# Moving weight splits, weight loads and the last norm of a hybrid decoder layer on one Trainium2 core

## The chip, the cores and the metric

The kernel runs on one core of one Trainium2 chip. TensorE (PE) does the matmuls; VectorE (DVE), ScalarE (ACT) and GpSimd (POOL) do elementwise work, each in the order of its own queue; SyncE (SP) issues most DMA transfers, also in queue order, so that whatever stands behind a waiting instruction waits too. The metric is the device time of one execution in microseconds (us). The kernel before took 1433.9 us, the median of 3 runs from 1433.82 to 1433.96.

## The reference

One decoder layer in float32, sequence S = 1024, width D = 1024, feed-forward width 2816, one batch. Cut to its frame (the details of the attention branches are left out):

```python
n1 = rms_norm(h, g_mix[i])
proj = n1 @ w_in[i]
...
mixed = jnp.concatenate([rms_norm(y_conv, g_gn_conv[i]), rms_norm(y_attn, g_gn_attn[i])], axis=-1)
h = h + mixed @ w_out[i]
u = causal_dwconv(rms_norm(h, g_ffn[i]) @ w_up[i], w_ffn_conv[i])
u_gate, u_val = jnp.split(u, 2, axis=-1)
h = h + (jax.nn.silu(u_gate) * u_val) @ w_down[i]
ple_gate = jax.nn.sigmoid(rms_norm(h, g_ple[i]) @ w_ple_gate[i])
h = h + ple_gate * (p[i] @ w_ple_proj[i])
return rms_norm(h, g_final)
```

`rms_norm` divides by the root of the mean square of a row and multiplies by a gain.

## The kernel before

Activations lie with the features on the partitions: eight tiles `hx0` to `hx7` of 128 features by 1024 tokens hold the residual stream, and a stage works on halves of 512 tokens. Every float32 product is made of three matmuls (`mm3`, lines 180 to 182): a high part times a high part and two mixed terms. Each weight and each moving operand is therefore *split* before use: ACT copies the high part (line 101) and DVE subtracts it from the original to get the low part (line 104). A split has two halves on two engines, and the second needs the first.

Weights come through a plan. `fetch` issues a load into a raw tile (line 147; line 142 for the weights `pt` of the last gate), `send` splits it, and `weights(key)` runs `send` a few keys ahead of use. The tiles come from pools with a fixed number of buffers per tag: `opool` has the tags `or` (raw) and `ot` (4 buffers, also used for temporaries), the feed-forward pool has `fp` pages, the general pool `pg` pages. A tile waits until the readers of the buffer's last holder are done. The program is written in the order of the calls, but a scheduler places each instruction on its engine's queue; `behind(a, b)` adds an edge, without a semaphore, that keeps a after b in that order.

The stages that matter, in order of time:

1. *Output product* (`oc` to 552 us, `oa` to 614 us). `conv_out` multiplies the convolution group by `out00` to `out07` (PE tile `oc`). `out_half(1)` and `out_half(0)` multiply the normalised attention group `yan` by `out10` to `out17` (PE tile `oa`, eight tiles for each half of the tokens, 12 matmuls each), DVE adds the result to `hx` (line 966), ACT and DVE take sums of squares (`facc`), and SP writes the half tile to DRAM (`hd`, line 968). `hold_out` splits `out1x` into one page `out1x_p` that holds both parts. Ahead of the loop stand loads and splits of the layer's embedding operands: `pT` (`ptr`, `pth`, `ptl`) and `w_pp` (`ppr`, `pph`, `ppl`). `norm0` is the group norm for the second half of the tokens; after its rsqrt (ACT `an0rr`, behind an ACT_TABLE_LOAD) come the four `yan0x` splits.
2. *Embedding* (614 to 638 us). `embed()` multiplies `pT` by `w_pp` in eight steps of 12 matmuls and parks the result in DRAM. After six steps the sum of the feed-forward norm (`fn0s`) goes to PE; its reciprocal and transpose on DVE give `fn0rb`.
3. *Feed-forward up* (636 to 1082 us). The products go by Strassen-like combinations: seven moving operands `m1` to `m7` (splits of sums and differences of the four normed quarters `x11`, `x12`, `x21`, `x22`) and, for each of the 22 column pairs j, seven weight combinations made by `up_weights(j)`: `ug` (products 1 and 2), `ut` (5 and 6), `us` (3 and 7), `uv` (4), with sums on DVE (lines 984 to 987). PE accumulates in `ua`, `ub`, `uc`, `ud`; `up(j)` convolves, applies SiLU and writes `ad`.
4. *Feed-forward down* (1062 to 1324 us, beginning between the last up products): PE tile `d`, weights `down0j` and `down1j`, 512 KB each, activations `a` read back from `ad`. The raw tiles of `pt` have buffers of the tags `or` and `ot`, which the up stage uses until its end.
5. *Gates* (1325 to 1417 us). Column gates `g` with weights `pg`, then for the last 256 tokens the gate `gl` by token with weights `pt`. The final norm of tokens 0 to 767 (`on`, generator `final`) is a sum, a rsqrt (ACT square root and DVE reciprocal unless its name is in `NEWTON`, where DVE does twelve small instructions), a transpose to `onrb`, and eight multiplications of `h` (line 1236) that each release an output DMA on POOL's queue (line 1237). The tokens 768 to 1023 (`hT6`, `hT7`) are finished by `gated` and `norm` (lines 1302 to 1327).

## Time and profile before

| | before |
|---|---|
| median of 3 runs | 1433.9 us |
| profiled execution, its own time | 1434.68 us |
| span of that execution | 1432.9 us |
| PE busy | 1379.8 us, 96% of the span |
| DVE, ACT, POOL busy | 927.4, 629.6, 130.5 us |
| mean granted TensorE clock | 0.985 of 2.4 GHz |

"Busy" counts executing instructions. A row of the trace gives start, duration, engine, line, operation, output<-input and shape; in square brackets stands the idle time of the engine just before it and what ended it. PEclk is the share of full speed that TensorE was granted. A share near 100% says which engine to look at, not where time can be had: that is read from the places where that engine stands still, and from what ends each wait.

### The profile page before, as it was taken

How to read it: one execution, taken by the hardware profiler on the slowest of the kernel's cores; microseconds unless marked ns; L12 is line 12 of the kernel's file. 1: busy time of each engine (PE TensorE's matmuls, PEld its weight loads, DVE VectorE, ACT ScalarE, POOL GpSimd, SP SyncE). 2: the span in 40 equal slices, each digit the busy share in tenths (PEclk: the TensorE clock that was granted, in tenths of full speed). 3: DMA queues.
4: the chain of work that ended last, by engine and by line, in shares of the span. 5: the costliest groups of instructions: out<-in, count | busy, mean ns of one | idle time of the engine just before them, and what ended most of it. 6: DMA issues, size and time to landing. Idle time of an engine off the chain costs nothing.

```text
span 1432.9 us, 17553 instructions
## 1 busy us (share of the span) xinstructions
PE 1379.8 (96%) x6527; PEld 1086.8 (76%) x6527; DVE 927.4 (65%) x1655; ACT 629.6 (44%) x1032; POOL 130.5 (9%) x147
## 2 busy tenths in 40 slices
...
GB/s 266 112 183 119 90 59 30 30 89 30 12 34 79 26 81 155 81 184 37 87 82 88 75 88 89 59 88 74 89 221 247 134 143 108 200 109 81 118 98 174
DMA packets 68773, 148.64 MB, mean 104 GB/s; under 512 B 6608, under 2 KB 28112, under 8 KB 68688
## 3 DMA queue, kind: packets, MB, share of 16 engines
...
q0 software_dynamic: 640, 3.15, 0.6%
...
## 4 chain that ended last, share of the span: by engine, by line
PE 87%; DVE 5%; DMA 3%; SPq 2%; ACT 1%; issue 1%; POOL 0%; DVEq 0%; POOLq 0%; ACTq 0%
PE d L180 6%; PE d L181 6%; PE d L182 6%; PE ua L182 4%; PE ua L181 4%; PE ua L180 4%; PE uc L182 3%; PE uc L181 3%; PE uc L180 3%; PE sy L755 2%; PE wy L755 2%; PE g L180 2%; PE g L182 2%; PE g L181 2%; PE ud L180 1%; PE ud L182 1%
## 5 line engine op out<-in xcount | busy, mean ns | idle before, releaser
L180 PE MATMUL d<-a,down_h 128*128 128x512 f32 x352 | 139.8, 398 | 4.4 <-ACT down_h L101 4.4
L181 PE MATMUL d<-a,down_h 128*128 128x512 f32 x352 | 139.5, 396 | 0.0
L182 PE MATMUL d<-a,down_l 128*128 128x512 f32 x352 | 136.5, 394 | 0.0
L104 DVE TENSOR_TENSOR down_l<-down_r,down_h 128x1024 fp32r<-128x1024 f32 x44 | 53.9, 1224 | 111.5 <-ACT down_h L101 68.0
L101 ACT ACTIVATE down_h<-down_r 128x1024 fp32r<-128x1024 f32 x44 | 46.7, 1061 | 137.1 <-DMA down_r<-in_w_down_dram 120.9
L1237 POOL DMA_DIRECT2D out_dram<-h x8 | 4.5, 564 | 865.0 <-DVE h L1236 864.8
L180 PEld LDWEIGHTS d<-a,down_h 128*128 128x128 f32 x352 | 66.7, 190 | 21.1 <-ACT down_h L101 5.2
L181 PEld LDWEIGHTS d<-a,down_h 128*128 128x128 f32 x352 | 66.7, 189 | 15.5
L182 PEld LDWEIGHTS d<-a,down_l 128*128 128x128 f32 x352 | 66.1, 188 | 15.7
L1143 ACT ACTIVATE uc<-xg,vec 128x1024 f32<-128x1024 f32 x22 | 25.3, 1151 | 107.1 <-DVE xg L1136 107.1
L1136 DVE TENSOR_TENSOR xg<-uc,e 128x512 f32<-128x512 f32 x22 | 15.2, 691 | 73.9 <-PE uc L182 73.7
L101 ACT ACTIVATE in_h<-in_r 128x1024 fp32r<-128x1024 f32 (+1 forms) x20 | 20.7, 1037 | 95.0 <-PE cx L181 30.1
L707 ACT ACTIVATE ps<-ps,stat 128x512 f32<-128x512 f32 (+7 forms) x64 | 49.1, 770 | 13.4 <-DVE stat L718 13.1
L104 DVE TENSOR_TENSOR in_l<-in_r,in_h 128x1024 fp32r<-128x1024 f32 (+2 forms) x22 | 25.0, 1140 | 28.8 <-ACT in_h L101 28.7
L180 PE MATMUL g<-gh,pg_h 128*128 128x512 f32 (+1 forms) x128 | 43.5, 340 | 0.0
L182 PE MATMUL g<-gh,pg_l 128*128 128x512 f32 (+1 forms) x128 | 43.2, 337 | 0.0
L181 PE MATMUL g<-gl,pg_h 128*128 128x512 f32 (+1 forms) x128 | 43.1, 337 | 0.0
L104 DVE TENSOR_TENSOR a<-a 128x512 fp32r<-128x512 f32 x44 | 28.8, 687 | 20.2 <-ACT a L101 20.0
L626 ACT ACTIVATE pw<-pw,stat 128x640 f32<-128x640 f32 (+3 forms) x56 | 38.2, 685 | 5.5 <-DVE stat L680 3.3
L101 ACT ACTIVATE uth<-ut 128x1024 fp32r<-128x1024 f32 x22 | 23.4, 1063 | 37.2 <-DVE ut L985 37.2
L180 PE MATMUL oa<-yan,out_p 128*128 128x512 f32 x64 | 28.0, 438 | 11.4 <-ACT out_p L101 6.3
L566 PE MATMUL s<-ks,qa 128*128 128x512 f32 (+3 forms) x96 | 36.5, 387 | 0.2 <-DVE stat L718 0.2
...
## 6 DMA issues: line engine op xcount, KB each, us to landing
down_r<-in_w_down_dram SPq DMA_DIRECT2D x44, 512.0 KB, 4.4
uvr<-in_w_up_dram SPq DMA_DIRECT2D x22, 512.0 KB, 3.6
ugr<-in_w_up_dram SPq DMA_DIRECT2D x22, 512.0 KB, 4.5
ad<-uc SPq DMA_DIRECT2D x22, 512.0 KB, 2.8
...
in_r<-in_w_in_dram SPq DMA_DIRECT2D x18, 512.0 KB, 7.1
qa<-qd SPq DMA_DIRECT2D x8, 512.0 KB, 4.8
...
```

What stands on the lines that cost most here:

```text
L101: nc.scalar.activation(hi, x, AF.Copy)
L104: (nc.gpsimd if (lo_eng or lo_of[0]) == "pool" else nc.vector).tensor_sub(lo, x, f32(hi))
L180: first = nc.tensor.matmul(ps, wh, mh, start=start, stop=False, **more)
L181: nc.tensor.matmul(ps, wh, ml, start=False, stop=False, **more)
L182: return first, nc.tensor.matmul(ps, wl, mh, start=False, stop=stop, **more)
L566: nc.tensor.matmul(ps[:, c0:c0 + n], b.qa[:, h, :], k, start=True, stop=False)
L626: nc.scalar.activation(w[:, :b.nw * P], w[:, :b.nw * P], AF.Exp, bias=b.M_W[:, h:h + 1], scale=-1.0, accum_out=b.D_W[:, h:h + 1])
L707: nc.scalar.activation(w[:, :nk], w[:, :nk], AF.Exp, bias=b.M_S[:, h:h + 1], scale=-1.0, accum_out=b.D_S[:, h:h + 1])
L755: m = nc.tensor.matmul(py[64 * g:64 * g + 64, :], vals(n, g), pts[g], start=n == 0, stop=n == nblk - 1)
L1136: nc.vector.tensor_add(xg[:, hi], c, e2)
L1143: nc.scalar.activation(u, xe[:, 0:S], AF.Copy, scale=col(tap))
L1237: nc.gpsimd.dma_start(out[k], o)
```

## The change

Line numbers in the rows are those of the program they belong to; lines of the changed kernel stand 0 to 19 higher.

1. `hold_out`: `out10` and `out11` go to four `ot` tiles (`out10_h`, `out10_l`, ...) in place of pages; `out12` to `out14` (before: `out10` to `out13`) use the feed-forward pool, the rest general pages.
2. The loads and splits of `pT` and `w_pp` are issued after two steps of `out_half(1)`, `norm0`'s first step and two more steps, where before they stood ahead of all of them.
3. `fetch` puts each `pt` load behind the last load issued for another weight (`sent_load`).
4. `up_weights` becomes a generator: first the loads and the split of `ug`, then the sums and the other splits. For pair 1 the second step is issued after all moving operands; for all other pairs both follow one another as before. The moving operands come in the order 6, 5, 7, 4, 3 (before 7, 6, 5, 4, 3) and differ in which temporaries they use.
5. `fn0s` is issued after four steps of `embed()` instead of six.
6. `final`: `on` joins `NEWTON`; the first step is issued behind the last column gate, the second (with its matmul behind the latest `gl` matmul) after the third `pt0` weight, the rest after the loop.

```diff
@@ -111,9 +111,13 @@
     def hold_out(key, raw):
 
         c = int(key[4:])
-        t = wpage([P, 2, 512], f"{key}_p", F32R) if c < 4 else page([P, 2, 512], f"{key}_p", F32R)
-        split(raw, t[:, 0], t[:, 1])
-        parts_of[key] = (t[:, 0], t[:, 1])
+        if c < 2:
+            parts = [opool[0].tile([P, 512], F32R, tag="ot", name=f"{key}_{u}", bufs=4) for u in "hl"]
+        else:
+            t = wpage([P, 2, 512], f"{key}_p", F32R) if c < 5 else page([P, 2, 512], f"{key}_p", F32R)
+            parts = [t[:, 0], t[:, 1]]
+        split(raw, *parts)
+        parts_of[key] = parts
 
     def split_gain(x, g, hi, lo):
         nc.scalar.activation(hi, x, AF.Copy, scale=g)
@@ -124,6 +128,7 @@
     order, src_of, raw_of, parts_of, got, sent = [], {}, {}, {}, [0], [0]
     hold = {"out00", "out10", "down00"}
     with_raw = {}
+    sent_load = [None]
 
     def plan(key, src, n):
         order.append(key)
@@ -139,12 +144,12 @@
             elif key.startswith("pt"):
                 raw = [opool[0].tile([P, 512], F32, tag=t, name=f"{key}_r{u}", bufs=b) for u, (t, b) in enumerate((("or", 2), ("ot", 4)))]
                 for u in range(2):
-                    load(raw[u], src[:, hs(u)])
+                    behind(load(raw[u], src[:, hs(u)]), sent_load[0])
                 raw_of[key] = raw
                 continue
             else:
                 raw = rawpage([P, n], f"{key}_r")
-            load(raw, src)
+            sent_load[0] = load(raw, src)
             raw_of[key] = raw
 
     def send(upto):
@@ -979,14 +984,16 @@
         load(v, w_up[2 * j + 1])
         load(g, w_up[2 * j])
         one, two = hs(0), hs(1)
+        gh_, gl_ = (wpage([P, S], f"ug{q}{j}", F32R) for q in "hl")
+        split(g, gh_, gl_)
+        ups[j] = {1: (gh_[:, one], gl_[:, one]), 2: (gh_[:, two], gl_[:, two])}
+        yield
         t = page([P, S], f"ut{j}")
         a7, a3 = (opool[0].tile([P, 512], F32, tag="or", name=f"u{q}s{j}", bufs=2) for q in "73")
         nc.vector.tensor_add(t[:, two], v[:, one], v[:, two])
         nc.vector.tensor_add(t[:, one], g[:, one], t[:, two])
         nc.vector.tensor_add(a7, g[:, one], v[:, one])
         nc.vector.tensor_add(a3, g[:, two], t[:, one])
-        gh_, gl_ = (wpage([P, S], f"ug{q}{j}", F32R) for q in "hl")
-        split(g, gh_, gl_)
         th_, tl_ = (wpage([P, S], f"ut{q}{j}", F32R) for q in "hl")
         split(t, th_, tl_)
         sh_, sl_ = (wpage([P, S], f"us{q}{j}", F32R) for q in "hl")
@@ -994,9 +1001,9 @@
         vp = wpage([P, S], f"uv{j}", F32R)
         split(v[:, two], vp[:, one], vp[:, two])
         split(a3, sh_[:, two], sl_[:, two])
-        ups[j] = {1: (gh_[:, one], gl_[:, one]), 2: (gh_[:, two], gl_[:, two]), 6: (th_[:, one], tl_[:, one]),
-                  5: (th_[:, two], tl_[:, two]), 7: (sh_[:, one], sl_[:, one]), 4: (vp[:, one], vp[:, two]),
-                  3: (sh_[:, two], sl_[:, two])}
+        ups[j].update({6: (th_[:, one], tl_[:, one]), 5: (th_[:, two], tl_[:, two]), 7: (sh_[:, one], sl_[:, one]),
+                       4: (vp[:, one], vp[:, two]), 3: (sh_[:, two], sl_[:, two])})
+        yield
 
     mov = {n: [None] * 4 for n in range(1, 8)}
 
@@ -1009,6 +1016,13 @@
         x = h[k][:, hs(hf)]
         nc.vector.scalar_tensor_tensor(x, x, col(V_FFN + k), rb, op0=ALU.mult, op1=ALU.mult)
         return x
+
+    half1, half0 = out_half(1), out_half(0)
+    next(half1)
+    next(half1)
+    next(norm0)
+    next(half1)
+    next(half1)
 
 
     pparts, wppt, wpp = [], [], []
@@ -1027,10 +1041,6 @@
         for c in range(4):
             wpp.append([[t[:, (2 * c + k) * P:(2 * c + k + 1) * P] for k in range(2)] for t in wppt[q]])
 
-    half1, half0 = out_half(1), out_half(0)
-    next(half1)
-    next(half1)
-    next(norm0)
     for _ in half1:
         pass
     res1 = []
@@ -1040,7 +1050,8 @@
         next(half0)
     next(norm1)
     x12, x22 = ([normed(k + 4 * q, 1, res1[0]) for k in range(4)] for q in range(2))
-    up_weights(0)
+    for _ in up_weights(0):
+        pass
     for _ in half0:
         pass
 
@@ -1073,7 +1084,7 @@
 
     mark = []
     steps = embed()
-    for _ in range(6):
+    for _ in range(4):
         next(steps)
     rb = rstd_rows([fsum[0]], D, "fn0", sums=lambda m: (behind(m, last[0]), mark.append(m)))
     for _ in steps:
@@ -1084,25 +1095,25 @@
     x21 = [normed(k + 4, 0, rb) for k in range(4)]
     for k in range(4):
         moving(2, k, x21[k])
-    up_weights(1)
-    for k in range(4):
-        t = temp(f"t7{k}")
-        nc.vector.tensor_sub(t, x22[k], x12[k])
-        moving(7, k, t)
-    x6 = []
+    second = up_weights(1)
+    next(second)
     for k in range(4):
         nc.vector.tensor_sub(x11[k], x11[k], x12[k])
-        t = x12[k]
+        t = temp(f"t6{k}")
         nc.vector.scalar_tensor_tensor(t, x11[k], -1.0, x22[k], op0=ALU.mult, op1=ALU.subtract)
         moving(6, k, t)
-        x6.append(t)
+        nc.vector.tensor_add(x21[k], x21[k], t)
     for k in range(4):
         moving(5, k, x11[k])
     for k in range(4):
-        nc.vector.tensor_add(x21[k], x21[k], x6[k])
+        nc.vector.tensor_sub(x12[k], x22[k], x12[k])
+        moving(7, k, x12[k])
+    for k in range(4):
         moving(4, k, x21[k])
     for k in range(4):
         moving(3, k, x22[k])
+    for _ in second:
+        pass
 
     def product(ps, j, n, start=True):
 
@@ -1158,7 +1169,8 @@
             next(run[j])
         next(run[j])
         if j + 2 < NF:
-            up_weights(j + 2)
+            for _ in up_weights(j + 2):
+                pass
         if j == NF - 2:
             hold.clear()
             send(order.index("down01") + 1)
@@ -1230,7 +1242,7 @@
     def final(acc):
 
         res = []
-        yield from rstd_steps(res, [acc], D, "on")
+        yield from rstd_steps(res, [acc], D, "on", sums=lambda m: behind(m, last[0]))
         for k in range(KC):
             o = h[k][:, 0:LAST]
             nc.vector.scalar_tensor_tensor(o, o, col(V_FIN + k), res[0], op0=ALU.mult, op1=ALU.mult)
@@ -1278,6 +1290,7 @@
                     nc.tensor.transpose(ps[:, k * P:(k + 1) * P], h[4 * q + k][:, toks[i]], ident)
                 nc.scalar.activation(hT[i][:, hs(q)], ps, AF.Copy)
     done = final(acc)
+    next(done)
 
 
     gfin = page([P, D], "gfin")
@@ -1294,7 +1307,7 @@
         for k in ks:
             o = (k % 2) * 512 + c0 % 512
             wh, wl = (t[0][:, o:o + n] for t in wgt[c0 // 512, k // 2])
-            mm3(ps, gh[k][:, toks[i]], gl[k][:, toks[i]], wh, wl, k == 0, k == KC - 1)
+            last[0] = mm3(ps, gh[k][:, toks[i]], gl[k][:, toks[i]], wh, wl, k == 0, k == KC - 1)[1]
 
     def gated(i, c0, n, pg, last):
         cs = slice(c0, c0 + n)
@@ -1332,6 +1345,8 @@
         wgt[0, kk] = weights(f"pt0{kk}", width=KC * P)
         for i in late:
             token_product(pgs[i], i, 0, 512, (2 * kk, 2 * kk + 1))
+        if kk == 2:
+            next(done)
     for kk in range(4):
         wgt[1, kk] = weights(f"pt1{kk}", width=KC * P)
     for i in late:
@@ -1340,19 +1355,17 @@
         for c0, n in pieces[i, 1]:
             pg = bank(f"gl{i}{c0}")[:, 0:n]
             token_product(pg, i, c0, n, range(KC))
-            if done:
-                for _ in done:
-                    pass
-                done = None
             used[i] = gated(i, c0, n, pg, (i, c0, n) == (late[-1], *pieces[i, 1][-1]))
             if i != late[-1]:
                 norm(i, used[i])
+    for _ in done:
+        pass
     norm(late[-1], used[late[-1]])
 
 
 LAST = 768
 GAP = (1, 4, 5)
-NEWTON = ("cn", "an1", "o6")
+NEWTON = ("cn", "an1", "on", "o6")
 OUT2 = (P, (S - LAST) // P, D)
 NPB, NPAGE, NWR, NWT, NFP, NPW, NHALF, AHEAD = 4, 29, 2, 8, 18, 13, 8, 3
```

How the queues move, from the order in which each program issues its instructions. First ACT at the start of the output product by `out10` to `out17`; `pth`, `pph` are high parts of `pT` and `w_pp`, `ugh0` the high part of the first up weight, `facc1` and `f11sq` squares, `an0rr` the rsqrt of `norm0`. Before:

```order
L101 ACTIVATE pth0_5077<-ptr0_5075 128x1024
L101 ACTIVATE pth1_5083<-ptr1_5081 128x1024
L101 ACTIVATE pph0_5089<-ppr0_5087 128x1024
L101 ACTIVATE pph1_5095<-ppr1_5093 128x1024
L101 ACTIVATE out10_p_5106<-out10_r_5100 128x512
L101 ACTIVATE out11_p_5109<-out11_r_5102 128x512
L101 ACTIVATE out12_p_5112<-out12_r_5104 128x512
L101 ACTIVATE out13_p_5133<-out13_r_5131 128x512
L210 ACTIVATE facc1_5099<-hx0_4116 128x512
L101 ACTIVATE ugh0_5388<-ugr0_5378 128x1024
L222 ACT_TABLE_LOAD
L222 ACTIVATE an0rr_5156<-an0s_5154,eps_83 128x16
```

The changed kernel, same engine and place:

```order
L101 ACTIVATE out10_h_5082<-out10_r_5076 128x512
L218 ACTIVATE ya01sq_5018<-ya1_2052 128x512
L218 ACTIVATE ya02sq_5021<-ya2_2053 128x512
L218 ACTIVATE ya03sq_5024<-ya3_2054 128x512
L101 ACTIVATE out11_h_5086<-out11_r_5078 128x512
L215 ACTIVATE facc1_5075<-hx0_4116 128x512
L101 ACTIVATE out12_p_5090<-out12_r_5080 128x512
L101 ACTIVATE out13_p_5111<-out13_r_5109 128x512
L227 ACT_TABLE_LOAD
L227 ACTIVATE an0rr_5134<-an0s_5132,eps_83 128x16
L218 ACTIVATE f11sq_5128<-hx1_4380 128x512
L101 ACTIVATE out14_p_5157<-out14_r_5155 128x512
```

The splits of `pT`, `w_pp` and `ugh0` have left the space ahead of `out14_p`; the split of `out14` has moved ahead of the `yan0x` splits.

Then DVE while the up stage starts; `m7x` is a low part of moving operand 7, `t7x` its difference, `ut1`, `u3s1`, `utl1`, `usl1` belong to the weights of pair 1. Before:

```order
L985 TENSOR_TENSOR ut1_5742<-ugr1_5739,ut1_5742 128x512
L1090 TENSOR_TENSOR t72_5776<-hx6_4970,hx2_4512 128x512
L1090 TENSOR_TENSOR t73_5781<-hx7_5031,hx3_4724 128x512
L1096 SCALAR_TENSOR_TENSOR hx0_4116<-hx0_4116,hx4_4812 128x512
L1096 SCALAR_TENSOR_TENSOR hx1_4380<-hx1_4380,hx5_4897 128x512
L104 TENSOR_TENSOR m70_5768<-t70_5766,m70_5768 128x512
L987 TENSOR_TENSOR u3s1_5744<-ugr1_5739,ut1_5742 128x512
L104 TENSOR_TENSOR m71_5773<-t71_5771,m71_5773 128x512
L1096 SCALAR_TENSOR_TENSOR hx2_4512<-hx2_4512,hx6_4970 128x512
L104 TENSOR_TENSOR utl1_5754<-ut1_5742,uth1_5753 128x1024
L1096 SCALAR_TENSOR_TENSOR hx3_4724<-hx3_4724,hx7_5031 128x512
L104 TENSOR_TENSOR m72_5778<-t72_5776,m72_5778 128x512
```

The changed kernel, where the first instruction for `ut1` stands:

```order
L104 TENSOR_TENSOR m30_5816<-hx4_4812,m30_5816 128x512
L104 TENSOR_TENSOR m31_5819<-hx5_4897,m31_5819 128x512
L104 TENSOR_TENSOR m32_5822<-hx6_4970,m32_5822 128x512
L104 TENSOR_TENSOR m33_5825<-hx7_5031,m33_5825 128x512
L993 TENSOR_TENSOR ut1_5828<-uvr1_5740 128x512
L994 TENSOR_TENSOR ut1_5828<-ugr1_5741,ut1_5828 128x512
L996 TENSOR_TENSOR u3s1_5830<-ugr1_5741,ut1_5828 128x512
L104 TENSOR_TENSOR utl1_5836<-ut1_5828,uth1_5835 128x1024
L104 TENSOR_TENSOR usl1_5840<-u7s1_5829,ush1_5839 128x512
```

The instructions for `ut1`, `u3s1`, `utl1` stood between those for the moving operands and now stand behind the last one, `m33`.

Last SP where the down stage starts; `a0xx` are activations read back, `ad<-uc120` writes those of pair 20, `downxx_r` are down weights. Before:

```order
L1173 DMA a018_9472<-ad_5072 128x512
L1149 DMA ad_5072<-uc119_8659 128x1024
L1173 DMA a019_9508<-ad_5072 128x512
L142 DMA pt00_r1_10923<-in_w_pt_dram 128x512
L142 DMA pt01_r1_11013<-in_w_pt_dram 128x512
L142 DMA pt02_r1_11090<-in_w_pt_dram 128x512
L142 DMA pt03_r1_11211<-in_w_pt_dram 128x512
L147 DMA down02_r_8924<-in_w_down_dram 128x1024
L1149 DMA ad_5072<-uc120_8784 128x1024
L147 DMA down03_r_8958<-in_w_down_dram 128x1024
L1173 DMA a020_9544<-ad_5072 128x512
```

The changed kernel:

```order
L1185 DMA a018_9474<-ad_5072 128x512
L1185 DMA a019_9510<-ad_5072 128x512
L1160 DMA ad_5072<-uc120_8786 128x1024
L152 DMA down02_r_8926<-in_w_down_dram 128x1024
L1185 DMA a020_9546<-ad_5072 128x512
```

The four `pt` loads have gone from here (they now stand behind the last column-gate weight `pg7_r`), and `down02_r` has moved from ahead of the write of pair 20 to behind it.

## Rows read from the trace of the kernel before

**Rows 1.** The page of the profile: busy time, share and instructions of each engine, and the chain of work that ended last, by engine.

```profile
PE 1379.8 (96%) x6527; PEld 1086.8 (76%) x6527; DVE 927.4 (65%) x1655; ACT 629.6 (44%) x1032; POOL 130.5 (9%) x147
PE 87%; DVE 5%; DMA 3%; SPq 2%; ACT 1%; issue 1%; POOL 0%; DVEq 0%; POOLq 0%; ACTq 0%
```

**Rows 2.** Waits of PE over the whole span, grouped: matmul tile and line, what ended the wait, then us in total, times, longest.

```profile
PE oa L180 <- ACT out_p L101: 6.3, 1, 6.3
PE oa L180 <- DVE hx L966: 5.0, 1, 5.0
PE d L180 <- ACT down_h L101: 4.4, 1, 4.4
PE uc L180 <- ACT m L101: 1.5, 1, 1.5
PE ud L180 <- ACT m L101: 1.1, 1, 1.1
```

**Rows 3.** Stretches of the span: its bounds and length, then busy us (and instructions) of PE, PEld, DVE, ACT, POOL, then PEclk, DMA share and GB/s.

```profile
558.00:563.20 5.20, 4.58 (x11) 3.63 (x12) 2.52 (x5) 1.72 (x4) 0.00 (x0) 0.50 0.35 104
577.40:580.00 2.60, 2.38 (x5) 1.13 (x5) 2.60 (x6) 1.56 (x4) 0.00 (x0) 0.50 0.26 101
580.00:600.00 20.00, 20.00 (x79) 16.06 (x80) 12.36 (x19) 4.95 (x8) 0.00 (x0) 0.90 0.29 105
650.00:655.00 5.00, 2.35 (x6) 1.26 (x6) 5.00 (x12) 3.43 (x7) 0.00 (x0) 0.71 0.52 186
655.00:680.00 25.00, 25.00 (x102) 20.12 (x101) 20.92 (x33) 10.12 (x16) 0.00 (x0) 0.92 0.02 4
1090.00:1095.00 5.00, 5.00 (x18) 3.95 (x18) 3.36 (x4) 2.26 (x3) 0.00 (x0) 0.76 0.81 273
1395.00:1418.00 23.00, 21.86 (x119) 18.62 (x118) 18.37 (x29) 14.10 (x25) 0.83 (x2) 1.00 0.30 107
1418.00:1433.00 15.00, 0.00 (x0) 0.00 (x0) 9.95 (x30) 3.13 (x7) 3.68 (x7) 0.57 0.74 280
```

**Rows 4.** Timeline of ACT in the output product: start, us, instruction, idle before it and what ended that.

```profile
552.86 1.06 ACT L101 ACTIVATE pth<-ptr 128x1024 fp32r<-128x1024 f32 x1 [4.60 <-DMA ptr<-in_pT_dram]
...
555.81 2.23 ACT L101 ACTIVATE pph<-ppr 128x1024 fp32r<-128x1024 f32 x2 [0.20 <-DMA ppr<-in_w_pp_dram]
557.95 1.13 ACT L101 ACTIVATE out_p<-out_r 128x512 fp32r<-128x512 f32 x2
...
568.49 1.06 ACT L101 ACTIVATE ugh<-ugr 128x1024 fp32r<-128x1024 f32 x1 [1.86 <-DMA ugr<-in_w_up_dram]
...
576.79 0.61 ACT L101 ACTIVATE out_p<-out_r 128x512 fp32r<-128x512 f32 x1
```

**Rows 5.** Timeline of DVE in the same place.

```profile
553.94 2.93 DVE L104 TENSOR_TENSOR ptl<-ptr,pth 128x1024 fp32r<-128x1024 f32 x2 [0.80 <-ACT pth L101]
556.90 2.40 DVE L104 TENSOR_TENSOR ppl<-ppr,pph 128x1024 fp32r<-128x1024 f32 x2
```

**Rows 6.** Timeline of PE: the last two matmuls before the wait that begins at 552.28 us.

```profile
551.65 0.39 PE L181 MATMUL oc<-ycl,out_h 128*128 128x512 f32 x1
551.89 0.39 PE L182 MATMUL oc<-ych,out_l 128*128 128x512 f32 x1
```

**Rows 7.** Timeline of DVE from the feed-forward norm to the up stage.

```profile
622.35 0.69 DVE L246 TENSOR_REDUCE fn0red<-fn0tr 128x16 f32<-128x512 f32 x1
...
627.92 0.25 DVE L223 RECIPROCAL fn0rr<-fn0rr 128x16 f32<-128x16 f32 x1 [4.88 <-ACT fn0rr L222]
...
634.26 3.09 DVE L104 TENSOR_TENSOR m<-hx,m 128x512 fp32r<-128x512 f32 x5
...
648.72 1.22 DVE L104 TENSOR_TENSOR utl<-ut,uth 128x1024 fp32r<-128x1024 f32 x1
```

**Rows 8.** Timeline of PE: the first matmul with weights `ut` of pair 0, behind the first four product tiles.

```profile
648.73 0.50 PE L180 MATMUL ua<-m,uth 128*128 128x512 f32 x1 [0.29 <-ACT e L1123]
```

**Rows 9.** Timeline of SP's queue where the down stage starts; the duration is that of issuing.

```profile
1073.38 9.59 SPq L142 DMA_DIRECT2D pt_r<-in_w_pt_dram  x4
1083.02 0.43 SPq L147 DMA_DIRECT2D down_r<-in_w_down_dram  x1
1083.78 0.33 SPq L1149 DMA_DIRECT2D ad<-uc  x1
```

**Rows 10.** The page, DMA issues: count, KB each, median us from issue to landing.

```profile
down_r<-in_w_down_dram SPq DMA_DIRECT2D x44, 512.0 KB, 4.4
```

**Rows 11.** Timeline of ACT: the split of that down weight.

```profile
1087.99 1.06 ACT L101 ACTIVATE down_h<-down_r 128x1024 fp32r<-128x1024 f32 x1 [3.15 <-DMA down_r<-in_w_down_dram]
```

**Rows 12.** Timeline of DVE in the place of rows 9.

```profile
1081.93 0.69 DVE L1136 TENSOR_TENSOR xg<-uc,e 128x512 f32<-128x512 f32 x1 [0.66 <-PE uc L182]
1082.54 1.22 DVE L1148 TENSOR_TENSOR uc<-uc,uc 128x1024 f32<-128x1024 f32 x1
```

**Rows 13.** Timeline of DVE in the tail.

```profile
1415.63 7.51 DVE L1236 SCALAR_TENSOR_TENSOR h<-h,vec,onrb 128x768 f32<-128x768 f32 x8
...
1427.29 0.16 DVE L233 SCALAR_TENSOR_TENSOR o6nb<-o6nb,o6nx 128x1 f32<-128x1 f32 x1
1427.49 0.16 DVE L234 SCALAR_TENSOR_TENSOR o6ny<-o6nb,o6ny 128x1 f32<-128x1 f32 x1
1427.68 0.48 DVE L1324 TENSOR_SCALAR hT<-hT,o6ny 128x512 f32<-128x512 f32 x1
```

## The prediction

> **What bounds the kernel now.** I read the page first. PE is busy in 96% of the span and carries 87% of the chain of work that ended last; DVE, the next, is busy in 65% [rows 1]. So time is to be had where PE stands still or runs slowly, and behind its last matmul. The waits of PE, grouped, come next [rows 2]: 6.3 us for the split of an output weight, 5.0 us in the same stage put down to DVE, 4.4 us for a down weight, and in the up stage 1.5 and 1.1 us for high parts of moving operands. Third, the windows around these waits [rows 3], for what a wait costs beyond itself. Behind the 6.3 us wait PE has 4.58 us of work at a granted clock of 0.50, which is the lower level, 1.2 of 2.4 GHz: 11 matmuls of 512 columns in 4.58 us are 0.42 us each, where one followed the other at 0.24 us (0.232 in the mean of longer stretches) before the wait [rows 6]. At 0.50 half of the busy time is loss, 2.3 us. The same for the others, busy time times (1 - clock): behind the 5.0 us wait 0.50 x 2.38 + 0.10 x 20 = 3.2 us; around the two up waits 0.29 x 2.35 + 0.08 x 25 = 2.7 us; behind the down wait 0.24 x 5 = 1.2 us and some 0.4 us between the end of the wait (1089.1) and the window's start. Last, PE does nothing in 1418 to 1433 while DVE works 9.95 of 15 us and the DMA engines are 74% busy [rows 3]: the tail is DVE work and output transfers.
>
> So the known stalls are worth: output stage 6.3 + 2.3 + 5.0 + 3.2 = 16.8 us; up start 1.5 + 1.1 + 2.7 = 5.3 us; down start 4.4 + 1.6 = 6.0 us. All 28 us would be the end of what can be won on PE.
>
> **Output stage (edits 1 and 2).** Why PE waits first: ACT stands still 4.60 us for the DMA of `pT`, does its splits, then the two `w_pp` splits (2.23 us), and only at 557.95 starts the first output weight, though PE was free at 552.28 [rows 4, 6]; DVE has 2.93 + 2.40 us of low parts in front of its own [rows 5]. In the changed kernel `out10` and `out11` are split before PE is through with `oc`, so this wait and its slow clock go. Why it waits a second time: `out14`'s split starts at 576.79, behind `ugh` (which waited for a transfer to 568.49), the rsqrt of `norm0` and the `yan` splits [rows 4]; the wait is named after DVE's `hx`, but `hx` was no more than what came last by the profile. In the new ACT order `ugh0` is far behind and `out14` ahead of the `yan` splits.
>
> The work does not vanish: `pT`, `w_pp` are 2 x 1.06 + 2.23 us on ACT and 5.3 us on DVE, and they now come between `out15` and `out17`. I laid the new queues out by hand with these durations, PE needing 12 x 0.232 = 2.8 us for one `oa` tile from 552.28. `out10` to `out13` come in time, the last narrowly, because `out12` stands behind a square that waits for the first finished `oa` tile. `out14`'s low part is some 0.3 us late (behind four `ya` multiplications and the transpose on DVE). `out15`'s low part stands behind two `yan` low parts, two `hx` additions and a sum: due at 567.0, ready at 569.5, 2.5 us. `out17`'s high part stands behind `pph1` and is some 1.2 us late. New waits 4.0 us. What they do to the clock the trace does not show: the waits of 5.0 and 6.3 us were followed by the lower level, and so were the two shorter ones of the up stage together. I take 0.9 us, a third of the loss around the two up waits, between none and 3.2 us as after the 5.0 us wait. Term: 16.8 - 4.0 - 0.9 = 11.9, taken as 12 us; ends 8 and 16.8.
>
> Other issue moved here: `ugr0`'s load stands on SP behind the write of the fifth half tile instead of ahead of the first. Its split is needed some 60 us later and costs nothing. Four `ot` buffers are taken by `out10`, `out11`; `out11` waits for the last `oc` tile of `out07`, which leaves it a whole `oa` tile (2.8 us).
>
> **Norm and up start (edits 4 and 5).** DVE has nothing to do for 4.88 us before the reciprocal at 627.92: its sum `fn0red` was done at 623.04, but `fn0s` stood on PE behind six embedding steps [rows 7]. Two steps are 12 matmuls of 512 and 12 of 256 columns, 12 x 0.232 + 12 x 0.118 = 4.2 us, so the norm comes 4.2 us earlier against PE, about when its sum is ready. With the output stage 12 us shorter DVE has less slack before the sum (in the two long windows of that stage it idled 5.20 - 2.52 and 20 - 12.36 us, 10.3 us together [rows 3], and the new order asks for some of it), so PE may now wait for the sum: I allow 0.8 us, ends 0 and 2.
>
> From then on DVE is full: in 650 to 655 it works 5.00 us, PE 2.35 [rows 3]. The normalisation ends at 634.26, and pieces follow at some 0.61 us each (five low parts in 3.09) [rows 7]. The sums and low parts of pair 1 (four sums, `utl1` of 1.22 us, `usl1` twice, `uv1`) are about 6 us in front of moving operands that PE wants first. Behind all of them now, they leave the operands 6 + 4.2 us earlier. The price is at the other end: PE wants `ut1` only 51 matmuls of pair 0 behind the first four tiles, which ended at about 648.4 [rows 8]: 648.4 + 51 x 0.232 = 660.2 in the old count. `utl1` is DVE's 48th piece behind the normalisation, which ends 4.2 us earlier at 630.1: 630.1 + 47 x 0.61 + 1.22 = 660.0, so with the sum's allowance it is one to one and a half late. Term: 5.3 - 1.3 = 4 us, ends 0 and 5.5.
>
> **Down start (edit 3).** SP spends 9.59 us on four `pt` loads, three of which wait for temporaries that DVE still reads (1081.93), and the down weight behind them goes out only at 1083.02 [rows 9, 12]; a down load lands after 4.4 us in the median [rows 10], this one after 4.97, when ACT's split begins [rows 11]. These loads go. But `down02_r` now stands behind the write of pair 20, which waits for the multiplication at 1082.54; that one came after `xg21`, which waited 0.66 us for PE [rows 12]. In the new order it stands ahead of `xg21`, and by my count it ends about 2 us earlier, at 1081.3 or so. 0.4 us for SP, 4.4 for landing, 1.06 for the split: 1087.2 against 1089.1. Term 1.8 us, ends -1.5 (same place on DVE as now) and 6.0 (write and load out in time). The `pt` loads come again behind `pg7_r`, some 40 us ahead of the first use: no term.
>
> **Tail (edit 6).** The eight multiplications take 7.51 us from 1415.63, ahead of the rest of `hT6` and `hT7`, and the last DVE step runs to 1428.16 [rows 13]. In the new order the sum, the rsqrt and the first multiplications stand ahead of the last token gates, so the first output DMAs leave earlier against PE's end, by my count some 5 us. But from 1418 to 1428.16 DVE works 9.95 of 10.16 us, so the tail is as long as DVE's list, and Newton's twelve steps at 0.20 us from start to start [rows 13] put 2.4 us on it, less one reciprocal of 0.25 (as in rows 7). Its idle time in 1395 to 1418 is 23 - 18.37 = 4.6 us [rows 3]; what the earlier sum and rsqrt fill of that shortens the tail. If none, 2.1 us are lost; if all, 2.5 gained. I take 0.5 us, with half a microsecond more at the lower end: ends -2.6 and 2.5.
>
> **Sum.** 12 - 0.8 + 4 + 1.8 + 0.5 = 17.5 us. The profiled execution took 1434.68, 0.8 above the median of 1433.9; its waits are taken as those of the median. 1433.9 - 17.5 = 1416.4; I forecast 1417, with the half microsecond for a layout by hand that leaves out semaphore delays.
>
> **The rivals.**
> (a) DVE becomes the bound of the output stage. Its 5.3 us for `pT` and `w_pp` and the `yan` parts are now in the midst of the tiles, so `out15`, `out16` and `out17` each wait 2 to 3 us and the clock falls: the stage gives 4 to 8 instead of 12, 1421 to 1425. For it: behind the second wait DVE works 2.60 of 2.60 us [rows 3]. Against: from 580 to 600 it works only 12.36 of 20 us [rows 3].
> (b) Slower. The waits left in the output stage hold PE at 1.2 GHz through it. A matmul of 512 columns costs 0.20 us more there (0.42 against 0.23, rounded up), the stage has 192 (half-stage 96). My forecast has about 4 of them slow; it takes 85 more for the gain of 17 to be gone, and 128 slow ones give 1417 + 25 = 1442. Against: the clock came back each time while PE had work without a break: 0.90 over 580 to 600 is 4 us more at the lower level and then full speed, 0.92 over 655 to 680 the same [rows 3].
> The Trainium skill has this as a rule ("TensorE: Matmul & The Clock Gate", section "A second HAM failure mode: psum-queue depth-cycling"): frequent short idle spells between groups of matmuls can make the clock swing between its two levels, which costs throughput although the engine looks busy. By that rule the new waits of 0.3, 2.5 and 1.2 us would bring (b); the trace agrees so far as the short waits of the up stage were followed by the lower level, and disagrees in that the level came back at once.
> (c) Down start as late as before, or worse, and a DVE tail with Newton in it 3 us longer: 1417 + 1.8 + 3.5 = 1422.
> (d) Better: the layout by hand is too dark, and the new waits of the output stage and the up start don't come. 16.8 + 5.3 + 1.8 + 0.5 = 24.4, with 0 to 4 more at the down start: 1405 to 1411.
>
> **Chances and range.** Forecast (1412 to 1421) 0.52; (a) 0.17; (c) 0.08; (d) 0.12; (b) 0.07; another 0.04 for gains that cancel near 1434. The range takes in the forecast, (a), (c) and the nearer part of (d), with 3 us more above for (a) and (c) together: 1409 to 1428. A measurement of this kernel can tell 0.2% from no change, 2.9 us: faster than 1431.0 0.89, within 1431.0 to 1436.8 0.04, slower 0.07.
>
> **What would show it.** Right: no wait of PE near the first `oa` matmul; one of 2 to 3 us at `out15`, PEclk at 1.00 over most of the output stage; DVE's idle time before the `fn0` rsqrt gone; no `pt_r` issue before the gates; eight output DMAs about 5 us nearer to PE's end. Wrong: a window of the output stage at 0.50 for over 10 us (b); waits of `oa` for `out_p` from DVE adding to more than 7 us (a); a down wait still above 4 us; a last output DMA issued later behind PE's end than now.

## The result and the profile after

The changed kernel took 1419.8 us, the median of 4 runs (1418.19 to 1420.25), beside 1433.93 us for the kernel before; the ratio is 0.9898, with a 95% interval from 0.9881 to 0.9915. The forecast was 1417, the range 1409 to 1428. Measured a second time, the same kernel took 1417.64 beside 1435.25 us (0.9881, 0.9866 to 0.9896). The experiments below are compared with this second measurement. Three of them (output stage undone, the `pt` loads free, the last norm undone) were taken together with it; the others have their own runs of the kernel before (medians 1435.77 and 1435.47 us), and for them a difference by the ratios stands beside that of the medians. An interval of such a ratio reaches some 2 us to either side, so small differences are read from stretches of the profile.

The profiled execution of the first measurement took 1418.19 us, with a span of 1416.4. The page, to be read beside [rows 1] (busy time of each engine, then the chain by engine):

```profile
PE 1372.7 (97%) x6527; PEld 1082.3 (76%) x6527; DVE 928.5 (66%) x1666; ACT 627.3 (44%) x1029; POOL 131.0 (9%) x147
...
PE 85%; DVE 6%; DMA 3%; ACT 2%; SPq 2%; issue 1%; POOL 0%; DVEq 0%; ACTq 0%; POOLq 0%
```

PE has 7 us less busy time though it issues the same 6527 matmuls: that is, for the most part, time it no longer spends at the lower clock (mean granted clock 0.991 instead of 0.985). DVE has 1 us more, the Newton steps. The rest of the gain is waiting time. The waits of PE, grouped, as in [rows 2]:

```profile
PE ua L185 <- ACT uth L101: 3.3, 1, 3.3
...
PE d L185 <- ACT down_h L101: 2.6, 1, 2.6
PE oa L185 <- ACT out_p L101: 2.5, 3, 1.3
PE oa L187 <- DVE out_p L104: 2.4, 2, 1.8
...
PE fn0s L256 <- DVE fn0red L251: 0.6, 1, 0.6
```

The two long waits for the output weights are gone; five short ones, 4.9 us in sum, stand in their place (predicted: 4.0). The down wait is 2.6 us (predicted: 2.6). The wait for `fn0red`, 0.6 us, was predicted with 0.8. One line is larger than predicted: 3.3 us at the up start for the high part `uth` of pair 1, where 1.3 were expected. The windows, to be read as [rows 3]:

```profile
551.00:613.00 62.00, 56.59 (x253) 44.83 (x252) 54.04 (x82) 29.76 (x49) 2.98 (x2) 1.00 0.55 188
650.00:655.00 5.00, 3.16 (x8) 2.45 (x9) 4.56 (x11) 3.57 (x5) 0.00 (x0) 0.73 0.00 0
1074.00:1080.00 6.00, 6.00 (x19) 4.77 (x20) 6.00 (x7) 3.60 (x4) 0.00 (x0) 0.72 0.55 221
1401.50:1412.02 10.52, 0.00 (x0) 0.00 (x0) 10.20 (x33) 6.04 (x14) 1.08 (x2) 0.74 0.44 170
```

PEclk is 1.00 over the output stage from its first `oa` matmul on, in spite of the five waits; it is 0.73 in the window of the up wait and 0.72 behind the down wait. The last window reaches from PE's end to DVE's end: 10.20 of 10.52 us, so the tail still is DVE's list, as in the kernel before.

The other signs that the prediction named: PE does not wait at the first `oa` matmul (551.48 us). The wait at `out15` is 1.75 us, under the 2 to 3 that were named. DVE's idle time before the `fn0` reciprocal is 0.80 us instead of the 4.88 of [rows 7]. The first `pt` load goes out at 1341.17 us, in the gates. The eight output DMAs of tokens 0 to 767 go out 5.4 to 6.0 us earlier against PE's end.

Where the time went, from the timeline of PE in both profiled executions (first and last matmul of a tile group):

| stretch | before | after | gain | predicted |
|---|---|---|---|---|
| start to first `oc` matmul | 460.70 | 459.41 | 1.3 | 0 |
| first `oc` to end of `oa` (output stage) | 153.97 | 143.41 | 10.6 | 12 |
| end of `oa` to end of `uc` (norm, embedding, up) | 467.22 | 465.74 | 1.5 | 3.2 |
| end of `uc` to end of `d` (down) | 242.95 | 240.98 | 2.0 | 1.8 |
| end of `d` to end of `gl` (gates) | 92.03 | 91.96 | 0.1 | 0 |
| end of `gl` to end of span (tail) | 16.03 | 14.90 | 1.1 | 0.5 |
| span | 1432.9 | 1416.4 | 16.5 | 17.5 |

The first row cannot be put down to the change: over all fourteen profiles of this study the first `oc` matmul lies between 458.47 and 461.01 us, with the kernel before (460.70) among the others and two executions of the changed kernel at 459.41 and 459.16.

### The profile page after: what moved, and what is told of

Its sections match the earlier page's. It is cut to its first block, busy times and chain, and to the rows that moved or that the text cites. A ratio compares the mean times of both kernels' runs of the same rounds, so it can differ in the third digit from the quotient of the medians.

```text
span 1416.4 us, 17575 instructions
## 1 busy us (share of the span) xinstructions
PE 1372.7 (97%) x6527; PEld 1082.3 (76%) x6527; DVE 928.5 (66%) x1666; ACT 627.3 (44%) x1029; POOL 131.0 (9%) x147
## 4 chain that ended last, share of the span: by engine, by line
PE 85%; DVE 6%; DMA 3%; ACT 2%; SPq 2%; issue 1%; POOL 0%; DVEq 0%; ACTq 0%; POOLq 0%
PE d L185 6%; PE d L186 6%; PE d L187 6%; PE ua L185 4%; PE ua L186 4%; PE ua L187 4%; PE uc L186 3%; PE uc L185 3%; PE uc L187 3%; PE sy L760 2%; PE wy L760 2%; PE g L185 2%; PE g L186 2%; PE g L187 2%; PE ub L187 1%; PE ub L185 1%
## 5 line engine op out<-in xcount | busy, mean ns | idle before, releaser
L1147 DVE TENSOR_TENSOR xg<-uc,e 128x512 f32<-128x512 f32 x22 | 15.2, 691 | 69.2 <-PE uc L187 69.1
L101 ACT ACTIVATE ugh<-ugr 128x1024 fp32r<-128x1024 f32 x22 | 23.4, 1061 | 36.4 <-DMA ugr<-in_w_up_dram 36.4
L185 PE MATMUL ua<-m,uth 128*128 128x512 f32 x88 | 35.2, 400 | 3.3 <-ACT uth L101 3.3
```

The costliest lines, as they stand in the source:

```text
L101: nc.scalar.activation(hi, x, AF.Copy)
L185: first = nc.tensor.matmul(ps, wh, mh, start=start, stop=False, **more)
L1147: nc.vector.tensor_add(xg[:, hi], c, e2)
```

## The experiments

Each diff is against the changed kernel if nothing else is said.

**The changed kernel again**

> The changed kernel once more, to see how far its executions differ. Theory: the gain of 14 to 16.5 us is there in each of them, 1418 to 1420.3, and the waits of PE are those of the first profile (output stage about 4.9 us in five waits, up start 3.3, down start 2.6). What differs lies ahead of the change (the first 120 us, where the first profile was already 1.3 us ahead of the kernel before). Rival: in the executions near 1420 the five new short waits of the output stage bring PE to 1.2 GHz for a while; a profile near 1420 then shows PEclk under 0.95 in a stretch of the output stage.

Measured: 1417.64 us (1417.1 to 1418.62). The waits are those of the first profile within 0.6 us, but the clock is not. In the output stage of this execution (the second line is where the down wait ends):

```profile
570.00:576.00 6.00, 5.16 (x14) 3.77 (x15) 6.00 (x9) 4.87 (x7) 0.00 (x0) 0.72 0.79 242
1074.40:1079.40 5.00, 4.98 (x21) 4.05 (x22) 5.00 (x6) 3.72 (x4) 0.00 (x0) 1.00 0.48 192
```

and in the first execution:

```profile
568.00:576.00 8.00, 4.38 (x18) 2.97 (x18) 8.00 (x11) 5.99 (x8) 0.00 (x0) 1.00 0.93 320
```

In the first profile PE went through the output stage at full clock and fell to the lower level behind the down wait of 2.63 us. Here it fell behind the output wait of 1.77 us (8 matmuls some 0.43 us apart) and stayed at 1.00 behind the down wait of 2.20 us. Its down stretch is 239.0 us long instead of 241.0, of which the wait explains 0.4. The theory had the place wrong: up to the first `oc` matmul the two executions differ by 0.25 us, behind it by up to 2.0. So the rival was half right: a part of the spread of one to two microseconds is the clock, but not in one place, and the execution with the lower clock in its output stage was the shorter of the two. In twelve profiles of this study the down wait is between 1.1 and 2.8 us. It was followed by the lower level at 2.31, 2.34, 2.38, 2.63, 2.75 and 2.78 us, and not at 2.48, 2.20 and four times at 1.15 to 1.18; the length of the wait alone does not decide it. The wait for `uth` at the up start says the same: it was followed by the lower level nine times at 3.17 to 3.31 us, and not in the one profile where it was 3.33 (the run with the embedding operands last, below).

**Output stage undone** (the output weights' tiles and the order of `out_half(1)` as before; the first hunk is in the function that splits an output weight)

```diff
-        if c < 2:
-            parts = [opool[0].tile([P, 512], F32R, tag="ot", name=f"{key}_{u}", bufs=4) for u in "hl"]
-        else:
-            t = wpage([P, 2, 512], f"{key}_p", F32R) if c < 5 else page([P, 2, 512], f"{key}_p", F32R)
-            parts = [t[:, 0], t[:, 1]]
-        split(raw, *parts)
-        parts_of[key] = parts
+        t = wpage([P, 2, 512], f"{key}_p", F32R) if c < 4 else page([P, 2, 512], f"{key}_p", F32R)
+        split(raw, t[:, 0], t[:, 1])
+        parts_of[key] = (t[:, 0], t[:, 1])
...
-    half1, half0 = out_half(1), out_half(0)
-    next(half1)
-    next(half1)
-    next(norm0)
-    next(half1)
-    next(half1)
...
+    half1, half0 = out_half(1), out_half(0)
+    next(half1)
+    next(half1)
+    next(norm0)
```

In the new place the second hunk's lines stand behind the loads and splits of `pT` and `w_pp`.

> Edits 1 and 2 undone together: out10 to out13 back in pages of the feed-forward pool, and the loads and splits of pT and w_pp ahead of the output product again; all else as changed. Theory (the output stage gives about 11 us): both long waits of oa come back with their slow clock, 1429 to 1432. Rival (what was won there would have been given back at the up start anyway, because DVE is the bound until 660 us): 1422 to 1426.

Measured: 1427.27 us (1426.72 to 1428.9), ratio 0.9948 (0.9936 to 0.9961). Both waits are back as in [rows 2]:

```profile
PE oa L181 <- ACT out_p L101: 6.6, 1, 6.6
PE oa L181 <- DVE hx L967: 5.6, 1, 5.6
```

The output stretch is 154.6 us, 10.5 to 11.2 longer than with the edits. The theory holds in the stage; the total is 1.7 us under the lower end of what was expected, and two things point that way: there is no wait for `fn0red`, and the down wait was 1.15 us here. The rival (given back at the up start) is out: the stretch from the end of `oa` to the end of `uc` is 465.9 us, as with the edits (465.7 and 466.1).

**One half of that change at a time**

First the tiles alone go back to pages; the order of issue stays that of the changed kernel. This is the first hunk above:

```diff
-        if c < 2:
-            parts = [opool[0].tile([P, 512], F32R, tag="ot", name=f"{key}_{u}", bufs=4) for u in "hl"]
...
+        t = wpage([P, 2, 512], f"{key}_p", F32R) if c < 4 else page([P, 2, 512], f"{key}_p", F32R)
```

> Edit 1 undone alone: out10 to out13 in feed-forward pages again, pT and w_pp still late. Theory: the order of pT ahead of the output weights was most of the first long wait, and the pages are free only when the last products of the convolution group are through; so PE waits 1.5 to 3 us at the first oa matmul instead of not at all, 1419 to 1422. Rival (the pages don't matter, the order does it all): no difference from the changed kernel (1417.6 in the same job as before).

Measured: 1424.27 us, ratio 0.9915 (0.9899 to 0.9932). Neither fits. The first `oa` tile loses only 0.6 us; the loss is further on, 3.92, 0.76 and 0.95 us for later output weights, and the output stretch is 148.0 us, 3.9 to 4.6 longer than in the changed kernel. On ACT the rsqrt of `norm0` stands later and both `w_pp` splits stand earlier, one of them, with the four `yan` splits, in front of `out14`'s split (the last line of ACT below), which the changed kernel has ahead of all of these:

```profile
565.25 1.06 ACT L101 ACTIVATE pph<-ppr 128x1024 fp32r<-128x1024 f32 x1 [0.99 <-DMA ppr<-in_w_pp_dram]
...
568.57 0.61 ACT L101 ACTIVATE out_p<-out_r 128x512 fp32r<-128x512 f32 x1
```

```profile
569.24 0.80 PE L181 MATMUL oa<-yan,out_p 128*128 128x512 f32 x1 [3.92 <-ACT out_p L101]
```

Why the scheduler orders them so with other pages, no run shows.

Then the order alone goes back, with `pT` and `w_pp` first; the tiles stay. This is the second hunk:

```diff
-    half1, half0 = out_half(1), out_half(0)
-    next(half1)
-    next(half1)
-    next(norm0)
-    next(half1)
-    next(half1)
...
+    half1, half0 = out_half(1), out_half(0)
+    next(half1)
+    next(half1)
+    next(norm0)
```

> Edit 2 undone alone: out10 and out11 in their own tiles, but pT and w_pp ahead of the output product again, and norm0 and the first up weight where they were. Theory: the first long wait goes, but out14 is still behind the up weight and the rsqrt on ACT, so that PE waits there as much longer as it came earlier: one wait of 8 to 12 us, 1425 to 1430, nearly as with both edits undone (1427.3). Rival (the two edits add, each taking away one wait): 1420 to 1423.

Measured: 1431.9 us, ratio 0.9971 (0.9961 to 0.9980). Two lines of ACT and one of PE:

```profile
562.71 1.06 ACT L101 ACTIVATE pth<-ptr 128x1024 fp32r<-128x1024 f32 x1 [4.69 <-DMA ptr<-in_pT_dram]
...
571.78 1.13 ACT L101 ACTIVATE out_p<-out_r 128x512 fp32r<-128x512 f32 x2
```

```profile
572.45 0.79 PE L185 MATMUL oa<-yan,out_p 128*128 128x512 f32 x1 [14.74 <-ACT out_p L101]
```

PE gets through the two tiles whose weights have their own place and then waits 14.7 us, longer than the two old waits together. `out12`'s split stands on ACT behind the rsqrt of `norm0`, `pT` (which waited 4.69 us for its transfer), `w_pp` and the `yan` splits. So there is one long wait, as the theory said, but two weights earlier than it said (`out12`, not `out14`), behind `pT` and not behind the up weight, and its 14.7 us and the total lie above the theory's ranges. The rival is out: the two edits don't add. Against the kernel with neither of them (1427.27), the new order alone is 3.0 us better (1424.27; by the ratios 4.7), the new tiles alone 4.6 us worse (1431.9; by the ratios 3.3), and both together 9.6 us better (1417.64).

**The embedding operands last** (all output weights of the half issued ahead of `pT` and `w_pp`, and the loads of these held behind earlier work)

```diff
     next(half1)
+    for _ in half1:
+        pass
...
-        load(t, pT[k])
+        behind(load(t, pT[k]), sent_load[0])
...
-        load(t, w_pp[q])
+        behind(load(t, w_pp[q]), sent_load[0])
...
-    for _ in half1:
-        pass
```

> The changed kernel with the loads of pT and w_pp behind the last output weight out17 and their splits behind its split. Theory: of the waits at oa those for the high parts of out16 and out17 (0.6 and 1.3 us, behind pph and pth on ACT) go, those for the low parts of out14 and out15 (0.6 and 1.8, behind the ya and yan work of norm0) stay: 1415.5 to 1417. Rival (DVE's amount of work, not its order, sets all these waits): the same sum of waits, 1417 to 1419, or the embedding products wait for pT instead.

Measured: 1425.06 us, ratio 0.9921 (0.9905 to 0.9938), 7.4 us above the changed kernel (5.7 by the ratios). The waits of `oa` did fall, to 2.7 us in sum, but PE waited 5.64 us somewhere neither theory had looked:

```profile
580.58 1.23 DVE L104 TENSOR_TENSOR ppl<-ppr,pph 128x1024 fp32r<-128x1024 f32 x1 [1.41 <-ACT pph L101]
...
583.11 1.23 DVE L104 TENSOR_TENSOR ppl<-ppr,pph 128x1024 fp32r<-128x1024 f32 x1 [0.70 <-ACT pph L101]
584.25 0.69 DVE L219 TENSOR_TENSOR facc<-facc,f17sq 128x512 f32<-128x512 f32 x1
...
591.25 0.68 DVE L251 TENSOR_REDUCE fn1red<-fn1tr 128x16 f32<-128x512 f32 x1
```

```profile
591.98 0.61 PE L256 MATMUL fn1s<-fn1red,same 128*128 128x16 f32 x2 [5.64 <-DVE fn1red L251]
```

DVE stood still for the high parts of `w_pp` (1.41 and 0.70 us), for whose transfers ACT waited, and the last square's sum, `facc`, and `fn1red` stood behind these splits. What is needed last was made to arrive last, and blocked, in a queue that runs in order, what was needed first.

**The four `pt` loads free again**

```diff
-                    behind(load(raw[u], src[:, hs(u)]), sent_load[0])
+                    load(raw[u], src[:, hs(u)])
```

> Edit 3 undone alone: the four pt loads may go out early again, two of them between the write of pair 20 and the down weight behind it. Theory: the wait of d for down_h goes from 2.6 back to over 4 us, 1421.5 to 1424. Rival (the 2 us at the down start come from the order of DVE around the write of pair 20, which this does not undo): no difference from the changed kernel by more than 0.7 us.

Measured: 1422.42 us (1420.16 to 1424.56), ratio 0.9912 (0.9897 to 0.9926): as the theory said. One `pt` load (two were expected) is back between the write of pair 20 and the down weight (SP's queue, then the split on ACT):

```profile
1069.77 0.33 SPq L1160 DMA_DIRECT2D ad<-uc  x1
1070.85 0.33 SPq L147 DMA_DIRECT2D pt_r<-in_w_pt_dram  x1
1071.27 0.41 SPq L152 DMA_DIRECT2D down_r<-in_w_down_dram  x1
```

```profile
1075.75 1.06 ACT L101 ACTIVATE down_h<-down_r 128x1024 fp32r<-128x1024 f32 x1 [2.70 <-DMA down_r<-in_w_down_dram]
```

The down weight's load goes out at 1071.27, 1.1 us later against the end of `uc` than in the changed kernel, and takes 4.5 us to land instead of 4.3; PE waits 3.98 us instead of 2.6 and 2.2. In the profile the down stretch is 242.2 us, 1.2 and 3.2 more than in the two profiles of the changed kernel; the 4.8 us between the medians are more than this stage shows, and the four runs reach from 1420.16 to 1424.56.

**Last norm undone, and Newton alone**

```diff
-        yield from rstd_steps(res, [acc], D, "on", sums=lambda m: behind(m, last[0]))
+        yield from rstd_steps(res, [acc], D, "on")
...
-    next(done)
...
+            if done:
...
-NEWTON = ("cn", "an1", "on", "o6")
+NEWTON = ("cn", "an1", "o6")
```

> Edit 6 undone alone: the last norm issued behind the first piece of the last gate, with ACT's square root. Theory (DVE's list sets the tail, the edit moves 2 us of it ahead of PE's end and adds 2 us of Newton steps): 0.5 to 1.5 us slower than the changed kernel, 1420.5 to 1421.5. Rival (the output DMAs set the tail, and they left 5 us earlier): 3 to 5 us slower.

Measured: 1420.42 us (1417.54 to 1421.08), ratio 0.9894 (0.9881 to 0.9908). The total cannot tell the two apart; the tail can: 16.05 us from PE's end to the span's end, as before the change (16.03), against 14.9 in both profiles of the changed kernel (14.9 to 15.6 in all eleven profiles with this tail). 1.1 us, as the theory said, although the eight output DMAs of tokens 0 to 767 leave 5.4 to 6.0 us later against PE's end: they are not what ends the kernel.

The second kernel keeps the early issue and only takes `"on"` out of `NEWTON`:

> Of edit 6 only Newton undone: the last norm is issued as early as in the changed kernel, but with ACT's square root and its table load. Theory (the 1.1 us of the tail come from the early issue; Newton's steps are as long as what they replace): from PE's end to the span's end 14.5 to 15.5 us as in the changed kernel (14.9), the time the same within noise. Rival (the table loads on ACT between the token gates were what the tail lost): 16 us or more.

Measured: 1417.21 us, ratio 0.9873 (0.9859 to 0.9888), and a tail of 13.8 us. Both expectations are wrong, on the same side. The DVE timeline of this kernel, then of the changed one:

```profile
1390.52 0.30 DVE L228 RECIPROCAL onrr<-onrr 128x24 f32<-128x24 f32 x1 [1.28 <-ACT onrr L227]
1390.86 0.98 DVE L261 STREAM_TRANSPOSE onrb<-onrr 128x768 f32<-128x768 f32 x1
...
1393.14 4.73 DVE L1248 SCALAR_TENSOR_TENSOR h<-h,vec,onrb 128x768 f32<-128x768 f32 x5
...
1410.45 0.49 DVE L1337 TENSOR_SCALAR hT<-hT,o6ny 128x512 f32<-128x512 f32 x1
```

```profile
1390.20 0.18 DVE L233 TENSOR_SCALAR onnx<-ons 128x24 f32<-128x24 f32 x1
...
1392.81 0.98 DVE L261 STREAM_TRANSPOSE onrb<-onny 128x768 f32<-128x768 f32 x1
...
1394.28 4.73 DVE L1248 SCALAR_TENSOR_TENSOR h<-h,vec,onrb 128x768 f32<-128x768 f32 x5
...
1411.54 0.48 DVE L1337 TENSOR_SCALAR hT<-hT,o6ny 128x512 f32<-128x512 f32 x1
```

PE ends at 1401.50 in both. With the square root DVE has `onrb` 1.95 us earlier and ends 1.1 us earlier. One difference ahead of the norm is not the cause: DVE's wait of 1.07 us for a transfer of `p` at 1382.77 us is nearly gone here (0.11), but it is also gone in the run with `pT` early again, whose tail is 14.9 us with Newton. So of edit 6 the early issue gives 2.2 us, and the Newton steps take 1.1 of it back.

**The up start: one step, six steps, another place**

```diff
-    next(second)
+    for _ in second:
+        pass
...
-    for _ in second:
-        pass
```

> Edit 4 undone in part: both steps of pair 1's weights ahead of the moving operands again (the new order 6, 5, 7, 4, 3 and the early norm of edit 5 stay). Theory (DVE is full there; where its 5 us for pair 1 stand only moves the wait from the products with uth of pair 1 to those with operands 6 and 5): the wait for uth goes, waits of 3 to 5 us for m come, and the time is that of the changed kernel within 1.5 us, 1416.5 to 1420. Rival (edit 4 as made is worth the 2.3 us that the up stage gained): 1420 to 1422.

Measured: 1414.65 us (1414.13 to 1415.75), ratio 0.9853 (0.9837 to 0.9870): 3.0 us faster than the changed kernel (4.0 by the ratios, whose intervals just touch), and neither expectation holds. In its own stretch, from the end of `oa` to the end of `uc`, it takes 464.1 us, 1.7 and 2.0 less than the changed kernel; the down stretch is 1.1 and 3.1 shorter, with a wait of 1.17 us and no fall of the clock. The wait for `uth` is gone, and the wait that takes its place is half of what was expected:

```profile
PE ud L185 <- ACT m L101: 1.5, 1, 1.5
```

```diff
-    for _ in range(4):
+    for _ in range(6):
         next(steps)
```

> Edit 5 undone alone: fn0s after six steps of the embedding again. Theory (DVE's chain from the norm to uth of pair 1 sets the up start): PE's wait for fn0red (0.6 to 1.2 us) goes, the reciprocal comes some 3.2 us later against PE, the waits behind it grow by 3 us, 1419.5 to 1421.5. Rival (the waits of the up start come from ACT's evacuations in the middle of the splits, not from the start of the chain): within 1 us of the changed kernel.

Measured: 1418.46 us, ratio 0.9881 (0.9866 to 0.9895), the same as the changed kernel, which is the rival's time and not the theory's. In its own stretch, however, it takes 468.1 us, 2.0 more than the 466.1 of the changed kernel in the second measurement; the down wait was 1.18 us without a fall of the clock and gave 0.8 back. What grew is not the wait for `uth`; a second wait came ahead of it:

```profile
PE ua L185 <- ACT uth L101: 3.2, 1, 3.2
PE ud L185 <- ACT m L101: 2.6, 1, 2.6
```

So in the stage the direction is the theory's, two thirds of its size.

```diff
+    for _ in second:
+        pass
     for k in range(4):
         moving(3, k, x22[k])
-    for _ in second:
-        pass
```

> The changed kernel with the second step of pair 1's weights issued ahead of moving operand 3 instead of behind it. In the changed kernel PE waits 3.3 us for uth of pair 1 while DVE stands still 3.5 us for high parts of operands 4 and 3 that ACT makes behind its evacuations of ua. Theory (order, not amount, of DVE's work sets this wait): the wait falls under 0.5 us and its slow clock goes, 1413 to 1414.5. Rival (DVE is the bound there, the wait moves to the products with operand 3): 1417 to 1418.5.

Measured: 1412.66 us (1411.83 to 1412.98), ratio 0.9835 (0.9818 to 0.9853), the fastest kernel of the study, 5.0 us faster than the changed kernel (6.6 by the ratios). No wait for `uth` is left; what remains of the lines looked at above is

```profile
PE oa L187 <- DVE out_p L104: 2.4, 2, 1.8
...
PE oa L185 <- ACT out_p L101: 1.3, 2, 1.0
PE d L185 <- ACT down_h L101: 1.2, 1, 1.2
```

and the window of the old wait is full at full clock:

```profile
642.00:655.00 13.00, 13.00 (x58) 10.51 (x57) 11.31 (x22) 6.25 (x10) 0.00 (x0) 1.00 0.05 21
```

The theory holds, with 0.3 us more than the range it gave: from the end of `oa` to the end of `uc` the kernel takes 460.4 us, 5.4 and 5.7 less than the changed kernel. What had made `uth` late shows in the changed kernel, on DVE and on ACT:

```profile
644.34 0.69 DVE L104 TENSOR_TENSOR m<-hx,m 128x512 fp32r<-128x512 f32 x1 [0.70 <-ACT m L101]
647.16 0.69 DVE L104 TENSOR_TENSOR m<-hx,m 128x512 fp32r<-128x512 f32 x1 [2.13 <-ACT m L101]
648.56 0.69 DVE L104 TENSOR_TENSOR m<-hx,m 128x512 fp32r<-128x512 f32 x1 [0.70 <-ACT m L101]
...
651.82 1.23 DVE L104 TENSOR_TENSOR utl<-ut,uth 128x1024 fp32r<-128x1024 f32 x1 [0.40 <-ACT uth L101]
```

```profile
646.01 0.60 ACT L1142 ACTIVATE e<-ua 128x512 f32<-128x512 f32 x1 [1.70 <-PE ua L187]
646.51 0.62 ACT L101 ACTIVATE m<-hx 128x512 fp32r<-128x512 f32 x1
...
650.73 1.06 ACT L101 ACTIVATE uth<-ut 128x1024 fp32r<-128x1024 f32 x1 [2.21 <-DVE ut L994]
```

DVE stands still 0.70, 2.13 and 0.70 us for high parts of the last moving operand. The longest of the three has its cause on ACT: the high part stands there behind `e`, an evacuation of `ua` that waits 1.70 us for PE. For the other two ACT had itself waited for DVE (1.16 and 0.76 us), and what held it is not shown. Behind these idle 3.5 us stands the first sum for pair 1. In the fast version DVE does that sum at 643.62 us, in what had been a gap.

**Splits of the embedding operands late, loads early** (from the kernel of the run above, and against it: the four loads stay where they were, their splits go behind all output weights and the second norm's start)

```diff
+    ptr = [rawpage([P, S], f"ptr{k}") for k in range(2)]
+    for k in range(2):
+        load(ptr[k], pT[k])
+    ppr = [rawpage([P, 8 * P], f"ppr{q}") for q in range(2)]
+    for q in range(2):
+        load(ppr[q], w_pp[q])
+    for _ in half1:
+        pass
...
+    next(norm1)
...
-        split(t, hi, lo)
+        split(ptr[k], hi, lo)
...
-        split(t, hi, lo)
+        split(ppr[q], hi, lo)
```

> The best version so far (pair 1 ahead of operand 3), with the loads of pT and w_pp where the changed kernel has them and their splits issued behind the first step of the norm fn1. The scheduler takes the splits of w_pp up as before and those of pT later. Theory (DVE's list between out14 and out17 sets the waits of oa, and 2.4 us of it go): waits of oa 2.5 to 3.5 us in sum instead of 3.7, no wait for fn1, 1410 to 1412.5. Rival (loads for later in front of out16 and out17 on SP's queue cost what is won): 1413 to 1418.

Measured: 1419.23 us (1417.55 to 1422.24), ratio 0.9889 (0.9872 to 0.9906), 6.6 us above the kernel it starts from (7.8 by the ratios, 0.0054 of 1435). Both expectations are wrong; the time lies above the rival's range too. In the output stage the wait for `out15` is gone, but the scheduler took both `w_pp` splits up ahead of the split of `out16` (the second line of ACT below), and ACT waited for their transfer. The load of `out16` is not what costs it: it goes out at 565.05 us, as in the changed kernel (565.25).

```profile
569.18 1.06 ACT L101 ACTIVATE pph<-ppr 128x1024 fp32r<-128x1024 f32 x1 [2.38 <-DMA ppr<-in_w_pp_dram]
...
571.61 0.61 ACT L101 ACTIVATE out_p<-out_r 128x512 fp32r<-128x512 f32 x1
```

```profile
572.28 0.80 PE L185 MATMUL oa<-yan,out_p 128*128 128x512 f32 x1 [4.17 <-ACT out_p L101]
```

This wait stands in the place of others, so the output stretch is only 0.9 us longer than in the run above. The profiled execution (1417.55 us) is 5.7 us longer than that of the run above (1411.83), and its other losses lie further on: 2.7 us from the end of `oa` to the end of `uc`, where PE waits 1.76 us for `fn0red` (0.24 in the run above) and falls to the lower level, and 2.5 us in the down stretch, where the wait is 2.31 us with a fall of the clock instead of 1.17 without. Whether the late splits cause these two waits is not shown.

## Why the prediction was right, and where not

**Output stage.** Named as the place where most would come from, and it was: 10.6 of 16.5 us, and 9.6 in the medians when undone. The sum of the new waits (4.9 against 4.0) and their places (`out14` and `out15` low parts, `out16` and `out17` high parts) came out nearly as laid out by hand. The 0.9 us of more waiting are balanced by the 0.9 us set aside for the clock, which were 0 in the first execution. That is luck: they were some 1.6 in the second, 8 matmuls at 0.43 instead of 0.23 us. Of the 1.4 us by which the term was too large, half a microsecond lies ahead of the `oa` tiles: the `oc` products wait 3.25 us for `ss`, where they waited 2.78. The rest is in no single line. Rival (a) is out: the stage gave 10 us, not 4 to 8. Rival (b), the slower one, happened in the small, 0 or 8 slow matmuls, a tenth of the 85 from which it would have decided.

**Norm and up start.** This is the term that was mis-sized: 4 - 0.8 us predicted, 1.5 measured (1.1 in the second measurement). The step that failed is "`utl1` is DVE's 48th piece behind the normalisation ... one to one and a half late". It counted DVE's pieces as if they followed one another without a break; DVE stood still 3.5 us among the last of them for ACT, and PE's wait was 3.3 us instead of 1.3. The direction of the credit was wrong too: the split of `up_weights(1)` into two steps was counted as the gain, but putting all of pair 1 ahead again, in one step, makes the stage 1.7 to 2.0 us shorter (and the kernel 3.0 us faster). What the stage won, it won by the earlier norm, 2.0 us; issued where edit 4 put it, the second step costs about what the norm gives, and one loop further up it gives 5.4 to 5.7 us.

**Down start.** 1.8 us predicted, 2.0 and 4.0 measured, the wait 2.63 and 2.20 us, where 4.4 less the term is 2.6. The chain was as described: the multiplication ends at 1068.17 in the new profile, 0.4 us ahead of the last `uc` matmul, then write, load and split:

```profile
1068.19 0.32 SPq L1160 DMA_DIRECT2D ad<-uc  x1
1068.60 0.38 SPq L152 DMA_DIRECT2D down_r<-in_w_down_dram  x1
```

```profile
1072.87 1.06 ACT L101 ACTIVATE down_h<-down_r 128x1024 fp32r<-128x1024 f32 x1 [1.34 <-DMA down_r<-in_w_down_dram]
```

The load landed in 4.3 us. What the term left out is that the clock may or may not fall behind a wait of this length.

**Tail.** 0.5 us predicted, 1.1 measured: inside its bounds (-2.6 to 2.5), and DVE's list was the right account, since the output DMAs, 5.4 to 6.0 us earlier against PE's end, shortened the tail by no more than 1.1 us. That Newton's steps cost in the tail what they take was in the working (2.1 us); 1.1 us of it show.

**The total.** 17.5 us in the sum, 16.5 in the profiled execution, of which 1.3 lie ahead of the change: so the edits gave 15.2, 2.3 less than the sum. In the medians the kernel gained 14.1 us in the first measurement and 17.6 in the second, and the sum lies between them. The output stage is short by 1.4 and the norm and up start by 1.7, the tail is over by 0.6. Rival (c) didn't come; of (d) only the experiment's version has come near (1412.66).
